# Sample attention of a hybrid decoder step: all scores of a pair of sequences ahead of its products with the values

## The chip, the cores and the metric

The kernel runs on one core of one Trainium2 chip. The metric is the device time of one execution in microseconds (us). A core has five engines with an instruction queue each: TensorE (PE in the profile, its weight loads are PEld), VectorE (DVE), ScalarE (ACT), GpSimd (POOL) and SyncE (SP, which only starts transfers here). POOL starts transfers too.

## What is computed

One step of a one-layer decoder trunk, for a prompt of 1024 tokens and for 8 sample sequences of 8 tokens each that have 2048 tokens of past. In the layer, gated linear attention stands beside sparse attention with three branches per query: compressed blocks, selected blocks and a sliding window. What matters here is the sparse attention of the samples, cut to its core:

```python
p_c = masked_softmax(q @ kc.T - slope * d_c, d_c >= 0)             # compressed blocks
o_c = p_c @ vc
idx = top_k(score_of_blocks(p_c), 16)                               # which blocks are selected
p_s = masked_softmax(q @ k_slc[idx].T - slope * d_s, d_s >= 0)      # selected blocks
o_s = p_s @ v_slc[idx]
p_w = masked_softmax(q @ k_win.T - slope * dist, 0 <= dist <= 512)  # banded keys
o_w = p_w @ v_win
o = gate_c * o_c + gate_s * o_s + gate_w * o_w
```

After it come the output projection, norms and a squared-ReLU MLP of width 4096.

## The kernel before

A first phase makes the conditioning vectors and compresses the keys and values of the samples' past. The main phase normalises, projects, runs the linear attention and then the sparse attention of the prompt in four parts of two tiles of 128 queries, in the order 1, 0, 2, 3. After it come the output projection and the MLP.

The prompt's attention (`branch` and `values` in the attention function) computes, per tile, group of heads and branch, scores on TensorE into the PSUM banks called "dn" (L1185, L1186), adds the mask and takes the maximum on VectorE (L1188), the exponential on ScalarE (L1192), scales on GpSimd (L1198), transposes the weights on TensorE into the banks called "g" (L1209), copies them out on ScalarE (L1211) and multiplies them with the values on TensorE (L1217).

The samples' attention is written out between these steps. `main_phase` keeps a generator, `between`, of sample work; after each piece of prompt work it takes from it until its share of 126 steps is reached. A number that the sample code yields is the weight of what it has just written. After part 2 all that is left is taken. Each instruction's place in its engine's queue is then fixed by the framework's scheduler when the kernel is built: it goes by the order in the program and by its own model of when each instruction is ready. At run time each engine works through its queue strictly in that order.

The samples are taken in four pairs. For a pair, the 128 rows are 2 sequences x 2 key heads x 4 query heads x 8 tokens. `sample_attention` loads for it the compressed values (vc, L1416), the banded keys and values (wk, L1418, and wv, L1420) and 32 pages of selected keys and values in eight units, two for each quarter q (`load_pages`, with the transfers at L247, half of them on SP's queue and half on POOL's). Then:

- the banded scores W (128 x 576): a product that writes the distances (L1362), four with the queries (L1364), the addition with the maximum on VectorE (L1374);
- their softmax (L1368 to L1371: a multiplication on VectorE, the exponential on ScalarE, two small operations on VectorE) and the scaling by the gate (L1433, L1434);
- the product of the compressed weights PC with vc, and of W with the banded values. `weigh` does each: transposes on TensorE into a bank (L1401), a copy to PT on ScalarE (L1403), products on TensorE (L1407) that add up in the bank `po`;
- the scores S of the selected blocks (128 x 2112) in four quarters of 512 and one rest of 64, each as for W, and their softmax with an exponential over 2112 columns;
- the products of S with the values, one rest and four quarters, into the other half of `po`;
- the sum of both halves, O (L1470, L1471), a transpose (L1473) and copies to `cats` (L1478).

All banks of the sample code come from the tag "mm", of which there are two. `po` holds one of them from its first product to O. The units for wk, wv and pages are nine slots that are taken in turn (seven of the weight buffers wr, wh and wl, and two called su): the banded keys of the next pair get the slot that the banded values of this pair leave, and the next banded values the slot of this pair's first page unit. vc has one buffer.

Of the kernel before, what the change touches and what calls it, by code (L numbers as in the profile page):

```python
# [223 lines left out]
class Prog:  # L224
# [6 lines left out]
    def t(self, pool, shape, dt=F32, tag=None, bufs=None):  # L231
        self.n += 1
        kw = {} if bufs is None else {"bufs": bufs}
        return pool.tile(list(shape), dt, name=f"{tag}_{self.n}", tag=tag, **kw)
# [104 lines left out]
    def C(self, name):  # L339
        o, n = self.at["cst"][name]  # L340
        return self.cst[:, o:o + n]
# [1035 lines left out]
    def sample_attention(self, pool):  # L1377
        nc, a, C = self.nc, self.a, self.C2
        t = lambda shape, tag, bufs=1, dt=F32: self.t(pool, shape, dt, tag, bufs)
        slots = cycle(["", "su", "", "", "", "su", "", "", ""])  # L1380


        def unit():
            return t([128, 1024], "su", 2) if next(slots) else self.raw_unit()


        def load_pages(pr, q):
            us = []
            for b2 in range(2):
                u = unit().rearrange("p (g n) -> p g n", g=4)  # L1390
                for g in range(4):
                    self.page_load(u[:, g], a["ckv"], (2 * pr + b2) * 16 + 4 * q + g, nc.gpsimd if g % 2 else nc.sync)
                us.append(u)
            return us

        def weigh(out, P, items, first, last):
            k = len(items)
            w = P.shape[1] // k
            pt = self.bank("mm")[:w, :128 * k]
            for g in range(k):  # L1400
                nc.tensor.transpose(pt[:, 128 * g:128 * g + 128], P[:, w * g:w * g + w], self.C("ident"))  # L1401
            PT = t([128, 512], "PT", 2)[:w, :128 * k]
            nc.scalar.copy(PT, pt)  # L1403

            for g, v in enumerate(items):
                for b2 in range(2):
                    nc.tensor.matmul(out[64 * b2:64 * b2 + 64], PT[:, 128 * g + 64 * b2:128 * g + 64 * b2 + 64], v(b2),  # L1407
                                     start=first and g == 0, stop=last and g == k - 1)

        lt = self.R2("l_t")  # L1410
        zero = C("zero")
        for pr in range(4):
            mx, sm = t([128, 3], "mxs", 2), t([128, 2], "sms", 2)
            new = self.R2("oh_tok")[:, 128 * pr:128 * pr + 128], self.R2("r_new")
            vc = t([128, 2, 128], "vc")
            nc.sync.dma_start(vc, self.vcs[2 * pr:2 * pr + 2].rearrange("b p c -> p b c"))  # L1416
            wk, wv = (unit().rearrange("p (b n) -> p b n", b=2) for _ in range(2))
            nc.sync.dma_start(wk, a["swk"][2 * pr:2 * pr + 2].rearrange("b p t -> p b t"))  # L1418
            wv = wv.rearrange("p b (g d) -> p b g d", g=4)
            nc.sync.dma_start(wv.rearrange("p b g d -> p (b g) d"),  # L1420
                              a["swv"][2 * pr:2 * pr + 2].rearrange("b (g p) d -> p (b g) d", p=128))
            pages = [load_pages(pr, q) for q in range(4)]

            W = t([128, 576], "Ws", 1)
            ps = self.bank("mm")
            self.scores(ps, pr, lambda b2: wk[:, b2], lt, self.R2("r_win"))
            self.add_max(W[:, :512], ps, zero.to_broadcast([128, 512]), None, mx[:, 0:1])
            ps = self.bank("mm")[:, :64]
            self.scores(ps, pr, lambda b2: self.kn[1], *new)
            self.add_max(W[:, 512:], ps, zero.to_broadcast([128, 64]), mx[:, 0:1], mx[:, 2:3])  # L1430
            yield 4
            self.softmax(W, mx[:, 2:3], sm[:, 1:2])
            nc.vector.tensor_tensor(sm[:, 1:2], sm[:, 1:2], self.G[:, pr, 2:3], op=OP.mult)  # L1433
            nc.vector.tensor_scalar(W, W, sm[:, 1:2], None, op0=OP.mult)  # L1434

            po = self.bank("mm")[:, :256].rearrange("p (a n) -> p a n", a=2)
            weigh(po[:, 1], self.PC[:, pr], [lambda b2: vc[:, b2]], True, False)
            yield 1
            weigh(po[:, 1], W[:, :512], [lambda b2, g=g: wv[:, b2, g] for g in range(4)], False, False)
            weigh(po[:, 1], W[:, 512:], [lambda b2: self.vn[1]], False, True)  # L1440
            yield 2

            S = t([128, 2112], "Ss", 1)
            pen = self.pen[:, pr]
            for q in range(4):
                ps = self.bank("mm")
                self.scores(ps, pr, lambda b2: pages[q][b2][:, :, :128], lt,
                            self.R2("r_slc")[:, None, :].to_broadcast([128, 8, 64]))
                self.add_max(S[:, 512 * q:512 * q + 512].rearrange("p (b i) -> p b i", i=64),
                             ps.rearrange("p (b i) -> p b i", i=64),  # L1450
                             pen[:, 8 * q:8 * q + 8, None].to_broadcast([128, 8, 64]),
                             mx[:, 0:1] if q else None, mx[:, 0:1])
                yield 2
            ps = self.bank("mm")[:, :64]
            self.scores(ps, pr, lambda b2: self.kn[0], *new)
            self.add_max(S[:, 2048:], ps, pen[:, 32:33].to_broadcast([128, 64]), mx[:, 0:1], mx[:, 1:2])
            self.softmax(S, mx[:, 1:2], sm[:, 0:1])
            nc.vector.tensor_tensor(sm[:, 0:1], sm[:, 0:1], self.G[:, pr, 1:2], op=OP.mult)
            yield 3
            weigh(po[:, 0], S[:, 2048:], [lambda b2: self.vn[0]], True, False)  # L1460
            for q in range(4):
                items = [lambda b2, q=q, g=g: pages[q][b2][:, g, 128:] for g in range(4)]
                weigh(po[:, 0], S[:, 512 * q:512 * q + 512], items, False, q == 3)
                yield 2
            O = t([128, 64], "O", 1)
            for b2 in range(2):
                for h in range(2):
                    s = slice(64 * b2 + 32 * h, 64 * b2 + 32 * h + 32)
                    c = slice(64 * h, 64 * h + 64)
                    nc.vector.tensor_scalar(O[s], po[s, 0, c], sm[s, 0:1], None, op0=OP.mult)  # L1470
                    nc.vector.tensor_tensor(O[s], O[s], po[s, 1, c], op=OP.add)  # L1471
            pt = self.bank("mm")[:64, :128]
            nc.tensor.transpose(pt, O, self.C("ident"))  # L1473
            for par in range(2):
                for b2 in range(2):
                    src = pt.rearrange("p (b h g r t) -> p b r (h g) t", b=2, h=2, g=2, r=2)[:, b2, par]
                    c = (2 * pr + b2) * 8
                    nc.scalar.copy(self.cats[64 * par:64 * par + 64, :, c:c + 8], src)  # L1478
            yield 1
# [349 lines left out]
```

## Time and profile before

| | |
|---|---|
| median of 3 runs | 1873.94 us (1870.25 to 1876.29) |
| the profiled execution | 1874.2 us |
| its span in the trace | 1872.5 us |
| PE busy | 1779.7 us, 95% of the span |
| DVE, ACT, POOL busy | 60%, 51%, 18% |
| mean granted TensorE clock | 0.976 of full speed |

The profile's page gives the busy time of each engine, then the span in 40 slices of 46.8 us. Its other views answer for a stretch: the busy time of each engine with the granted clock, the instructions in order of time, who waited for whom, and groups of instructions by line and shape. TensorE's clock has two levels, 1.2 and 2.4 GHz; a granted clock of 0.50 in a stretch is the lower one throughout, 1.00 the higher. A PE that is busy at the lower level does about half the work.

### The profile page before, as it was taken

What the parts mean: (1) busy time and instruction counts of PE and PEld (TensorE: products, weight loads), DVE (VectorE), ACT (ScalarE), POOL (GpSimd) and SP (SyncE); (2) the same over time, 40 slices, a digit from 0 to 9 for tenths busy, and PEclk for the clock granted to TensorE, in tenths of its full rate; (3) what the DMA queues carried; (4) which work ended last, traced back from release to release, by engine and by line L of the source; (5) the groups of instructions that cost most, each with busy time, mean ns of one, the idle gap of its engine ahead of it and who ended that gap; (6) DMA issues with size and microseconds to landing.
All of it is one profiled execution on the core that took longest, in us unless ns stands there. A gap on an engine that the chain in (4) does not pass through costs nothing.

```text
span 1872.5 us, 33307 instructions
## 1 busy us (share of the span) xinstructions
PE 1779.7 (95%) x12054; PEld 1626.9 (87%) x12054; DVE 1130.4 (60%) x2528; ACT 952.0 (51%) x1931; POOL 334.6 (18%) x502
## 2 busy tenths in 40 slices
PE   5899989999999999998998899999999999999998
PEld 4688889999989766665796899999999999999998
DVE  6777866474434764554636566855656569665555
ACT  5334445364233767664846556643443365654454
POOL 3534210012401446443312000000000001000000
PEclk9999999999999988998999899999999999999999
DMA  7777451013455513323222366321112145564442
GB/s 247 250 250 255 155 165 58 24 47 129 147 199 174 162 60 99 95 83 113 72 67 85 114 193 202 101 90 57 59 66 90 57 159 184 193 208 152 151 147 96
DMA packets 116779, 246.04 MB, mean 131 GB/s; under 512 B 14443, under 2 KB 71581, under 8 KB 115814
## 3 DMA queue, kind: packets, MB, share of 16 engines
q1 hardware_dynamic: 101046, 197.04, 33.0%
q0 software_dynamic: 13328, 43.99, 6.9%
q10 hardware_dynamic: 2240, 2.88, 0.4%
q8 instruction: 95, 1.56, 0.3%
q14 instruction: 70, 0.57, 0.1%
HBM read 215.94 MB, written 32.05 MB: 132 GB/s over the span
## 4 chain that ended last, share of the span: by engine, by line
PE 76%; DVE 8%; DMA 7%; ACT 3%; issue 3%; SPq 1%; POOL 1%; POOLq 0%; DVEq 0%; ACTq 0%
PE mm L261 11%; PE mm L262 11%; PE mm L263 11%; PE dn L261 5%; PE dn L262 5%; PE dn L263 5%; PE g L1209 3%; PE g L262 3%; PE g L263 3%; PE g L261 3%; PE av L1217 3%; DMA xt<-xT 2%; PE dn L1185 2%; PE dn L1186 2%; PE mm L1407 1%
## 5 line engine op out<-in xcount | busy, mean ns | idle before, releaser
L256 DVE TENSOR_TENSOR wl<-wr,wh 128x1024 fp32r<-128x1024 f32 x174 | 212.9, 1225 | 204.3 <-ACT wh L255 202.8
L255 ACT CAST wh<-wr 128x1024 fp32r<-128x1024 f32 (+1 forms) x176 | 183.3, 1043 | 241.0 <-PE mm L262 106.9
L261 PE MATMUL dn<-fh,wh 128*128 128x384 f32 (+1 forms) x616 | 205.0, 334 | 2.9 <-DVE fo L1627 1.7
L262 PE MATMUL dn<-fl,wh 128*128 128x384 f32 (+1 forms) x616 | 204.0, 331 | 0.0
L263 PE MATMUL dn<-fh,wl 128*128 128x384 f32 (+1 forms) x616 | 203.8, 332 | 0.0
L261 PE MATMUL mm<-hT,wh 128*128 128x384 f32 (+1 forms) x384 | 129.0, 336 | 11.3 <-ACT zq L778 5.2
L262 PE MATMUL mm<-hT,wh 128*128 128x384 f32 (+1 forms) x384 | 127.4, 332 | 0.0
L263 PE MATMUL mm<-hT,wl 128*128 128x384 f32 (+1 forms) x384 | 126.8, 332 | 0.4 <-DVE wl L256 0.4
L261 PEld LDWEIGHTS dn<-fh,wh 128*128 128x128 f32 x616 | 116.2, 189 | 5.5 <-DVE fo L1627 2.9
L262 PEld LDWEIGHTS dn<-fl,wh 128*128 128x128 f32 x616 | 116.3, 189 | 0.3 <-DVE fl L256 0.3
L263 PEld LDWEIGHTS dn<-fh,wl 128*128 128x128 f32 x616 | 116.1, 189 | 0.1
L1627 DVE TENSOR_TENSOR fo<-fo,dn 128x384 f32<-128x384 f32 (+1 forms) x134 | 72.4, 541 | 56.3 <-PE dn L263 56.0
L1211 ACT COPY pw<-g 128x512 f32<-128x512 f32 x148 | 80.7, 586 | 46.1 <-PE g L1209 45.6
L607 POOL TENSOR_TENSOR rs_r<-rs_m,mhalf 128x2 f32<-128x2 f32 (+2 forms) x11 | 11.2, 1019 | 483.3 <-DVE rs_m L606 483.3
L261 PE MATMUL mm<-w1h,wh 128*128 128x256 f32 x256 | 76.7, 300 | 17.7 <-ACT wh L255 16.1
L1185 PE MATMUL dn<-KK,QS 128*128 128x512 f32 (+3 forms) x192 | 77.7, 409 | 11.6 <-DVE mx L1188 10.9
L261 PEld LDWEIGHTS mm<-hT,wh 128*128 128x128 f32 x384 | 73.1, 190 | 14.3 <-ACT zq L778 5.6
L261 PE MATMUL mm<-cth,wh 128*128 128x256 f32 (+1 forms) x256 | 76.9, 302 | 5.3 <-ACT cth L255 5.2
L263 PE MATMUL mm<-x2h,wl 128*128 128x320 f32 x256 | 79.2, 309 | 0.0
L261 PE MATMUL mm<-x2h,wh 128*128 128x320 f32 x256 | 79.2, 309 | 0.0
L262 PE MATMUL mm<-x2l,wh 128*128 128x320 f32 x256 | 79.1, 309 | 0.0
L262 PE MATMUL mm<-ctl,wh 128*128 128x256 f32 (+1 forms) x256 | 76.6, 300 | 0.1
(643 smaller groups left out, 5444.3 us busy)
## 6 DMA issues: line engine op xcount, KB each, us to landing
wr<-w_up SPq DMA_DIRECT2D x72, 512.0 KB, 3.6
wr<-w_down SPq DMA_DIRECT2D x72, 512.0 KB, 3.6
wr<-w_ada SPq DMA_DIRECT2D x48, 512.0 KB, 5.1
wr<-w_f SPq DMA_DIRECT2D x24, 512.0 KB, 3.8
wr<-cw SPq DMA_DIRECT2D x16, 512.0 KB, 5.2
wr<-w_out SPq DMA_DIRECT2D x16, 512.0 KB, 3.5
raw<-cc SPq DMA_DIRECT2D x62, 128.0 KB, 4.8
raw<-cc POOLq DMA_DIRECT2D x61, 128.0 KB, 5.3
```

What stands on the lines that cost most here:

```text
L255: return (self.nc.scalar.copy(h, src), (lo or self.nc.vector).tensor_tensor(l, src, h.bitcast(F32), op=OP.subtract))
L256: (lo or self.nc.vector).tensor_tensor(l, src, h.bitcast(F32), op=OP.subtract))
L261: mm(out, ah, bh, start=start, stop=False)
L262: mm(out, ah, bl, start=False, stop=False)
L263: mm(out, al, bh, start=False, stop=stop)
L1185: nc.tensor.matmul(ps, q, K[:, 0, c:c + cw], start=True, stop=False)
L1186: nc.tensor.matmul(ps, q, K[:, 1, c:c + cw], start=False, stop=True)
L1209: nc.tensor.transpose(pt[:, 128 * g:128 * g + 128], S[g][:, c:c + 128], self.C("ident"))
L1211: box["group"].append((V, pw, nc.scalar.copy(pw, pt)))
L1217: m = nc.tensor.matmul(box["av"][64 * j:64 * j + 64], V, pw.rearrange("p (a j q) -> p j a q", a=2, j=2)[:, j], start=box["first"], stop=en ...
L1407: nc.tensor.matmul(out[64 * b2:64 * b2 + 64], PT[:, 128 * g + 64 * b2:128 * g + 64 * b2 + 64], v(b2), start=first and g == 0, stop=last an ...
L1627: nc.vector.tensor_tensor(o, o, ps, op=OP.add)
```

## The change

Seven lines move. The bank `po` is taken, and the products of the compressed weights and of the banded weights with their values are written, only after the softmax of the selected blocks' scores, right ahead of the products of S with the values. The scores S of a pair so come directly behind its banded scores and their softmax. No instruction is added or removed, and the weights that are yielded stay the same; only their order changes.

```diff
             nc.vector.tensor_scalar(W, W, sm[:, 1:2], None, op0=OP.mult)
 
-            po = self.bank("mm")[:, :256].rearrange("p (a n) -> p a n", a=2)
-            weigh(po[:, 1], self.PC[:, pr], [lambda b2: vc[:, b2]], True, False)
-            yield 1
-            weigh(po[:, 1], W[:, :512], [lambda b2, g=g: wv[:, b2, g] for g in range(4)], False, False)
-            weigh(po[:, 1], W[:, 512:], [lambda b2: self.vn[1]], False, True)
-            yield 2
-
             S = t([128, 2112], "Ss", 1)
             pen = self.pen[:, pr]
             for q in range(4):
...
             self.softmax(S, mx[:, 1:2], sm[:, 0:1])
             nc.vector.tensor_tensor(sm[:, 0:1], sm[:, 0:1], self.G[:, pr, 1:2], op=OP.mult)
             yield 3
+
+            po = self.bank("mm")[:, :256].rearrange("p (a n) -> p a n", a=2)
+            weigh(po[:, 1], self.PC[:, pr], [lambda b2: vc[:, b2]], True, False)
+            yield 1
+            weigh(po[:, 1], W[:, :512], [lambda b2, g=g: wv[:, b2, g] for g in range(4)], False, False)
+            weigh(po[:, 1], W[:, 512:], [lambda b2: self.vn[1]], False, True)
+            yield 2
             weigh(po[:, 0], S[:, 2048:], [lambda b2: self.vn[0]], True, False)
             for q in range(4):
```

## Rows read from the trace of the kernel before

**Rows 1.** Page: busy time of PE; busy tenths and clock in 40 slices.
```profile
PE 1779.7 (95%) x12054; PEld 1626.9 (87%) x12054; DVE 1130.4 (60%) x2528; ACT 952.0 (51%) x1931; POOL 334.6 (18%) x502
...
PE   5899989999999999998998899999999999999998
...
PEclk9999999999999988998999899999999999999999
```

**Rows 2.** Stretches: length, then busy us (instructions) of PE, PEld, DVE, ACT, POOL; clock; DMA.
```profile
715.00:735.00 20.00, 18.80 (x105) 15.10 (x103) 11.99 (x66) 17.65 (x59) 9.46 (x20) 0.66 0.05 14
...
800.00:815.00 15.00, 12.97 (x95) 9.16 (x97) 10.95 (x51) 9.06 (x29) 11.40 (x20) 1.00 0.53 159
```

**Rows 3.** The same view in steps of 5 us at the fourth pair's scores.
```profile
860.00:865.00 5.00, 1.87 (x18) 0.88 (x14) 2.82 (x7) 1.23 (x3) 4.70 (x6) 1.00 0.42 135
865.00:870.00 5.00, 3.46 (x25) 2.90 (x26) 0.68 (x3) 0.84 (x2) 0.00 (x0) 0.63 0.14 46
870.00:875.00 5.00, 5.00 (x18) 2.29 (x17) 0.23 (x1) 0.00 (x0) 0.00 (x0) 0.50 0.33 107
875.00:880.00 5.00, 5.00 (x29) 2.48 (x28) 1.65 (x8) 2.64 (x5) 0.00 (x0) 0.84 0.01 2
...
885.00:890.00 5.00, 4.04 (x25) 2.96 (x23) 3.59 (x16) 2.65 (x4) 1.06 (x3) 1.00 0.00 0
890.00:895.00 5.00, 3.68 (x19) 2.34 (x19) 3.93 (x17) 4.93 (x12) 0.93 (x2) 1.00 0.01 3
```

**Rows 4.** Order of time, POOL, DVE and ACT, fourth pair: start, length, instruction, idle before.
```profile
853.23 2.12 POOL L247 DMA_DIRECT2D wr<-ckv  x4
...
859.74 3.88 POOL L1198 TENSOR_SCALAR Ss<-Ss,sm,gates 128x768 f32<-128x768 f32 x4
...
861.55 2.07 DVE L1368 TENSOR_TENSOR mxs<-mxs,cols 128x1 f32<-128x1 f32 x1
...
863.57 1.13 POOL L247 DMA_DIRECT2D wl<-ckv  x2
...
863.66 0.87 ACT L1369 ACTIVATE Ws<-Ws,mxs,cols 128x576 f32<-128x576 f32 x1 [1.87 <-DVE mxs L1368]
...
865.23 0.52 DVE L1434 TENSOR_SCALAR Ws<-Ws,sms 128x576 f32<-128x576 f32 x1
```

**Rows 5.** Order of time, PE: banded values of the first pair, then the fourth pair.
```profile
701.64 1.09 PE L1407 MATMUL mm<-su,PT 128*64 128x128 f32 x16
...
865.81 0.66 PE L1401 MATMUL mm<-cst,Ws 128*128 128x128 f32 x4 [3.52 <-DVE Ws L1434]
867.19 1.97 PE L1407 MATMUL mm<-wr,PT 128*64 128x128 f32 x16 [0.73 <-ACT PT L1403]
...
883.73 0.50 PE L1362 MATMUL mm<-cstr 128*128 128x512 f32 x1
...
884.65 0.59 PE L1364 MATMUL mm<-wl,Q 128*64 128x512 f32 x1
```

**Rows 6.** Waits, 690 to 925 us: total us, times, longest; PE, then its weight loads.
```profile
PE mm L1401 <- DVE Ws L1434: 3.5, 1, 3.5
...
PEld mm L1362 <- DVE mxs L1374: 0.4, 1, 0.4
```

**Rows 7.** Groups by line and shape, 690 to 925 us: count, busy us, mean ns, idle.
```profile
L1374 DVE CUSTOM_DVE_ANT_1 Ss<-mm,pen,mxs 128x512 f32<-128x512 f32 x12 | 9.0, 751 | 19.6 <-PE mm L1364 19.6
...
L1369 ACT ACTIVATE Ss<-Ss,mxs,cols 128x2112 f32<-128x2112 f32 x4 | 8.6, 2142 | 0.0
```

**Rows 8.** Instructions on the tile mxs: ns min/median/max, first and last start.
```profile
L1368 DVE TENSOR_TENSOR mxs<-mxs,cols x8: 150/156/2072, 695.7 to 887.5; 128x1 f32<-128x1 f32 x8
```

**Rows 9.** Transfers issued, 690 to 925 us: count, size of one, median us to landing.
```profile
wl<-ckv POOLq DMA_DIRECT2D x12, 128.0 KB, 4.1
```

**Rows 10.** Order of time: the second pair's banded keys, on SP, then their scores, on DVE.
```profile
703.56 0.40 SPq L1418 DMA_DIRECT2D su<-swk  x1
...
751.89 0.69 DVE L1374 CUSTOM_DVE_ANT_0 Ws<-mm,cols 128x512 f32<-128x512 f32 x1 [1.23 <-PE mm L1364]
```

## The prediction

> **What bounds the kernel now.** I read the page's busy times first: PE is busy 1779.7 of 1872.5 us [rows 1]. So an edit that moves work without removing any can only pay where PE stands still or runs at its lower clock, 1.2 GHz. The page's slices say where that is: near the start, and around the 16th to 23rd slice, some 700 to 1075 us, where PE's tenths and its clock dip [rows 1]. The softmaxes of the four pairs of samples start between 695.7 and 887.5 us [rows 8], inside that part. Three views of it follow. The stretches show how much PE lacks: 2.03 of 15 us at 800 to 815, a granted clock of 0.66 at 715 to 735 [rows 2], and, at the fourth pair, 4.67 idle us between 860 and 870 and a lower clock up to about 877 [rows 3]. The waits give names: the longest wait of PE on a sample operation is one of 3.5 us, of the transposes of W for the scaled W; on the bank of the scores it waits 0.4 us in all [rows 6]. The order of time shows how the 3.5 us arose [rows 4, 5]: the small multiplication L1368 took 2.07 us, the exponential of W 0.87, the scaling 0.52, and PE, whose next instruction was the transpose of W, stood from 862.3 to 865.8. The clock then fell: sixteen products that took 1.09 us in the first pair took 1.97 [rows 5].
>
> **The change part by part.**
>
> *What moves.* Per pair 6 transposes, 24 products and 3 copies go from ahead of the selected scores to behind their softmax. At 1.09 us for sixteen products [rows 5] the 30 PE instructions are about 2.0 us of PE per pair. None is added, so PE's sum stays.
>
> *The fourth pair's wait.* With the change the next sample work behind the banded scores is the selected scores, which need neither the softmax of W nor `po`. A quarter takes PE 1.51 us (883.73 to 885.24) [rows 5]. With `po` not yet taken, two banks are free once W's two additions are done, before 861.55, so two quarters, 3.0 us, fit into the hole at once; the last of their pages were issued on POOL from 853.23 on [rows 4]. The hole is 10 - 1.87 - 3.46 = 4.67 us [rows 3]. Bounds: 3.0 to 4.67 gained if they start at once, 0 if they don't. I take 3.8, between the two quarters and the whole, because a third can follow once L1368 is over (863.62) and one addition of 0.75 done [rows 4, 7], from 864.4 on.
>
> *The lower clock behind it.* The share at 1.2 GHz is twice what the clock lacks: 3.7, 5.0 and 1.6 us of the three steps from 865, 10.3 us in all [rows 3]. 0.73 of it is idle [rows 5]; the other 9.6 at the ratio 1.97 / 1.09 = 1.81 would take 5.3, so 4.3 us are at stake. Bounds 0 (the clock falls anyway) to 4.3. I take two thirds, 2.9: what went before the fall was the hole, and some of a hole may stay.
>
> *The wait for the exponential of S.* It takes 2.14 us [rows 7], and around the fourth pair's PE idles 0.96 + 1.32 = 2.28 us [rows 3]. The moved products, 2.0 us, now lie ready there. But these gaps are short waits of the prompt's scores for their banks. Bounds 0 to 2.0; I take 0.7.
>
> *A new wait.* The copy of the compressed weights to PT stood beside the exponential of W (0.87 us); now it may stand behind that of S (2.14). Behind it on ACT queue the prompt's copies L1211 and exponentials; on PE the products L1407 wait for it, and all prompt work behind them. Bounds 0 to 2.14 per pair. I take 0.5 in all: the copies of the banded weights showed waits of that size [rows 5].
>
> *Three other pairs.* Their W softmax has no long wait on PE (the 3.5 us is one wait of one) [rows 6], so taking the weights away from there gains nothing. Scores of 1.51 us PE per 0.75 us DVE [rows 5, 7] fill PE as well as the products did: 0, bounds -1 to +1 us.
>
> *The first pair's slow clock.* From 715 to 735 us the lower level covers 13.6 us, but ACT is busy 17.65 of 20 us [rows 2], so a full clock could give back at most 2.35 us. Bounds 0 to 2.35; I take 0, as the exponentials of the prompt stay.
>
> *Two banks.* The selected scores now alternate between two. The row says that PE waited 0.4 us for that bank [rows 6], since prompt work fills the time: 0. The Trainium skill, "Perfetto Trace Analysis", section "Optimizing Tensor Performance", asks that independent groups rotate through different banks, so that taking one out overlaps the next; were each wait exposed, the time would be that of the second rival below, and the row speaks against it.
>
> *Queues.* The next pair's banded keys wait for the slot of this pair's banded values. In the first pair they were issued at 703.56 and used only at 751.89 [rows 10]. They will now be issued behind the selected scores, some 20 us later, which leaves over 20 us of cover. Behind them on SP stands the load of the next banded values, which waits for the products of S with the values anyway. The next vc is loaded later by as much and used later by as much. POOL's page loads keep their order. Cost 0; without the cover it would be a landing, some 4 us [rows 9].
>
> **The sum**, against the profiled execution of 1874.2 us (0.3 above the median of the runs shown, span 1872.5, 1.7 outside it): -3.8 - 2.9 - 0.7 + 0.5 = -6.9, so 1867.3; I say 1867. What is gained at 865 us reaches the end if the stages behind stay bound by PE, which the slices of nine tenths and the clock near one say [rows 1].
>
> **The rivals.**
>
> *The hole moves.* The 2.07 us of L1368, against a median of 0.156 [rows 8], end at 863.62, as does POOL's scaling that began at 859.74 [rows 4]. That doesn't go away, and the additions for the selected scores now stand behind it on DVE. Two quarters run, the third from 864.4 to 865.9. The last quarter's page was issued on POOL behind the same scaling, the second of two at about 864.1; with 4.1 us to landing [rows 9] it is there at 868.3. PE then lacks sample work for 2.4 us, where it lacked it for 3.5, and the clock falls as before: -1.1 - 0.7 + 0.5, so 1873. The prompt's work can't fill it at once, as part 2's last weights are scaled on POOL until 863.62 [rows 4] and have to be transposed, copied and multiplied after that. By the Trainium skill, "SBUF — State Buffer", section "Who interferes with whom", a VectorE operation with two SBUF inputs and a GpSimd operation that reads SBUF shut each other out for a whole instruction; by that rule the trace agrees, with the 2.07 us.
>
> *Every bank wait was exposed.* Sixteen scores, four per pair, wait for the addition before them, 0.75 us each [rows 7]: 12 us, so 1862. For it speaks that DVE waited 19.6 us in these additions for PE [rows 7], so the chain of scores is in series; against it the 0.4 us [rows 6].
>
> *Slower: copies behind the long exponential.* If the scheduler puts the copy of the compressed weights behind the exponential of S in ACT's queue and the products next on PE, each pair costs 2.14 us [rows 7]: 8.6 us. It decides from the point where PE has no prompt work between the two. With the 3.8 us kept and the clock not: 1874.2 + 8.6 - 3.8 = 1879.0, and 1882.8 if the hole stays. For it: ACT is the busiest engine in the first pair, 17.65 of 20 us [rows 2]; against: the queue is laid out with a model of these times, and the longest such wait now is 0.73 us [rows 5].
>
> **How the numbers follow.** Forecast 0.47 (its own range 1861 to 1872), the hole moves 0.28, exposed banks 0.07, slower 0.18. A measurement of this kernel can tell about 0.3%, 5.6 us, from no change, so faster is below 1868.3 us. Two thirds of the forecast's chance lie there, 0.31, with the exposed banks and a rest of the second case 0.41; same 0.41; slower 0.18. Range: at the low end all bounds of the forecast, 4.67 + 4.3 + 2.0 + 2.35 = 13.3, so 1861; at the high end the slower case between its two prices, 1881.
>
> **What would show it.** Right: in the fourth pair PE goes from the banded scores to selected scores without a wait over 1 us, the wait of the transposes of W for L1434 is gone, the granted clock stays near 1.00 where it was 0.63, 0.50 and 0.84, and the pair ends earlier. Wrong: a wait of PE at L1407 or L1401 for PT copies behind L1369; a wait for a page; another stretch of lower clock elsewhere, since the queues of all engines are laid out anew from the first pair on, and a shift of a prompt tile against a pair may open a hole that no row of before shows.

## The result, and the profile after

The changed kernel takes 1864.66 us (median of six runs, 1863.48 to 1869.22), the kernel before 1875.84 beside it (six runs, 1870.25 to 1876.69). The ratio is 0.9945, 95% interval 0.9928 to 0.9961: 10.3 us less, 7.3 to 13.5. The forecast was 1867; the profiled execution fell from 1874.2 to 1863.61 us, by 10.6, where the sum said 6.9. From here on, us of a ratio are of 1876. One of the ten runs of an experiment below, with the banded products alone moved, took 3833.66 us and is left out of every figure.

The page after, its rows of PE and of the granted clock:

```profile
span 1862.0 us, 33308 instructions
...
PE 1773.2 (95%) x12054; PEld 1618.1 (87%) x12054; DVE 1128.9 (61%) x2528; ACT 950.3 (51%) x1931; POOL 339.7 (18%) x502
...
PE   5999989999999899999998899999999999999998
...
PEclk9999999999999999999999999999999999999999
```

The same 12054 matmuls keep PE busy 6.5 us less than before [rows 1]. No work went, so I put this down to the clock, though the profile doesn't separate it from other causes; two profiles with the same order of instructions, below, differ by up to 2.6 us in it. The other 4.0 of the 10.5 us of span are idle time. The eights in the clock's row are gone. The stretches that the prediction read, after (length, busy us of PE, PEld, DVE, ACT, POOL, clock, DMA):

```profile
715.00:735.00 20.00, 18.88 (x148) 14.61 (x150) 10.80 (x61) 18.02 (x67) 12.41 (x25) 0.91 0.18 57
800.00:815.00 15.00, 15.00 (x95) 8.53 (x94) 8.04 (x37) 6.76 (x19) 7.76 (x13) 1.00 0.23 73
...
850.00:855.00 5.00, 5.00 (x27) 2.11 (x25) 4.17 (x18) 3.54 (x10) 4.51 (x6) 1.00 0.30 90
855.00:860.00 5.00, 5.00 (x28) 2.56 (x24) 3.92 (x15) 2.15 (x4) 0.00 (x0) 1.00 0.10 33
860.00:865.00 5.00, 5.00 (x33) 2.82 (x32) 2.37 (x9) 4.47 (x8) 0.72 (x1) 1.00 0.02 5
865.00:870.00 5.00, 4.35 (x34) 2.65 (x32) 1.45 (x7) 2.17 (x5) 3.15 (x4) 1.00 0.00 0
870.00:875.00 5.00, 4.98 (x50) 3.48 (x49) 0.00 (x0) 3.48 (x8) 0.00 (x0) 1.00 0.32 107
```

Two things differ from [rows 2, 3]. Around the fourth pair's scores PE has no hole and the clock stays at 1.00. And at the first pair, where I had booked nothing, the granted clock is 0.91 and not 0.66: 3.4 us at the lower level (by the same view in steps of 5 us) in place of 13.6. PE in order of time at the fourth pair, and the exponentials that belong to it on ACT:

```profile
849.78 0.47 PE L1362 MATMUL mm<-cstr 128*128 128x512 f32 x1
850.18 1.08 PE L1364 MATMUL mm<-wl,Q 128*64 128x512 f32 x4
...
852.49 0.39 PE L1362 MATMUL mm<-cstr 128*128 128x512 f32 x1
```

```profile
853.54 0.87 ACT L1369 ACTIVATE Ws<-Ws,mxs,cols 128x576 f32<-128x576 f32 x1
...
863.82 2.15 ACT L1369 ACTIVATE Ss<-Ss,mxs,cols 128x2112 f32<-128x2112 f32 x1
```

The first selected quarter starts at 852.49, ahead of the exponential of W. From the one exponential to the other it is 10.3 us; before it was 25.0 (863.7 to 888.7). In the other three pairs it was 21.2, 23.6 and 27.8 and is 16.4, 14.4 and 12.6. The waits of PE after, 690 to 925 us (total, times, longest):

```profile
PE dn L1185 <- DVE mx L1188: 3.1, 7, 0.8
PE g L1209 <- POOL Ss L1198: 1.8, 4, 0.6
PE g L1209 <- POOL Sw L1198: 1.6, 2, 1.4
PE mm L1473 <- DVE O L1471: 1.4, 1, 1.4
PE mm L1407 <- ACT PT L1403: 0.3, 1, 0.3
```

The transposes of W wait no more [rows 6]. New are 3.4 us behind GpSimd's scaling of the prompt's weights. Two more rows, the small multiplications and the additions of the selected scores with their idle time before them:

```profile
L1368 DVE TENSOR_TENSOR mxs<-mxs,cols x8: 158/158/197, 695.3 to 863.6; 128x1 f32<-128x1 f32 x8
```

```profile
L1374 DVE CUSTOM_DVE_ANT_1 Ss<-mm,pen,mxs 128x512 f32<-128x512 f32 x12 | 9.0, 750 | 10.4 <-PE mm L1364 10.4
```

The 2072 ns of [rows 8] are gone, and DVE waits 10.4 us for scores where it waited 19.6 [rows 7].

### The profile page after: what moved, and what is told of

Same layout as the page of the kernel before. It is cut to its first block, busy times and chain, and to the rows that moved or that the text cites. A ratio compares the mean times of both kernels' runs of the same rounds, so it can differ in the third digit from the quotient of the medians.

```text
span 1862.0 us, 33308 instructions
## 1 busy us (share of the span) xinstructions
PE 1773.2 (95%) x12054; PEld 1618.1 (87%) x12054; DVE 1128.9 (61%) x2528; ACT 950.3 (51%) x1931; POOL 339.7 (18%) x502
## 4 chain that ended last, share of the span: by engine, by line
PE 75%; DMA 9%; DVE 7%; ACT 3%; issue 2%; POOL 2%; SPq 1%; POOLq 0%; DVEq 0%; ACTq 0%
PE mm L261 11%; PE mm L262 11%; PE mm L263 11%; PE dn L261 5%; PE dn L262 5%; PE dn L263 5%; PE av L1217 3%; PE g L263 3%; PE g L262 3%; PE g L261 3%; PE g L1209 3%; DMA xt<-xT 2%; PE dn L1185 2%; PE mm L1364 2%; PE dn L1186 1%
```

## Experiments

All were timed beside the kernel before. One profile can lie up to 6 us from its kernel's median, so the profiles are read for what they hold, and the times for what it is worth.

### One part of the pairs only

The new order in the fourth pair alone, in the first three, in the first, in the second and third: the moved lines stand twice, under a condition.

```diff
+            if not (pr == 3):
                 po = self.bank("mm")[:, :256].rearrange("p (a n) -> p a n", a=2)
...
             yield 3
+            if pr == 3:
+                po = self.bank("mm")[:, :256].rearrange("p (a n) -> p a n", a=2)
...
```

> Only the fourth pair has the new order; the first three keep the old one, and all queues up to the fourth pair are those of before. If the gain is the fourth pair's hole and the lower clock behind it (my theory): most of it is here, 6 to 9 us faster than before (near 1868), and the wait of the transposes of W for L1434 is gone. If the gain comes from the first three pairs (earlier ends of the pairs, the first pair's slow clock): 0 to 2 us.

> Only the first three pairs have the new order; the fourth has the old one. My theory: the hole of the fourth pair stays, so 0 to 3 us faster than before (1873 to 1876). If the gain comes from pairs that end earlier against the prompt's work: most of the 10 us, and no hole although the fourth pair's order is the old one.

> Only the first pair has the new order. In the first batch the new order in the first three pairs alone gave the whole gain (0.9948), and in its trace the lower clock at the first pair was gone (0.6 in place of 13.6 us of it behind 700 us) and the fourth pair's hole too. New theory: the first pair's lower clock is worth some 5 us, in spite of a busy ACT, and the first pair's own order ends it: 4 to 6 us faster than before, under 4 us of lower clock between 700 and 740, hole of the fourth pair unchanged. If ACT bounds that stretch, as predicted: 0 to 2.4 us.

> Only the second and third pairs have the new order. If they bring the fourth pair earlier against the prompt's tiles and its hole closes by that: 4 to 5 us faster, no idle stretch behind the fourth pair's banded scores, and the first pair's lower clock of 10 to 14 us stays. If they do nothing by themselves: within 1 us of before.

| new order in | median us | ratio, 95% interval | us |
|---|---|---|---|
| fourth pair | 1870.30 | 0.9978 (0.9961 to 0.9996) | -4.1 |
| first three | 1864.80 | 0.9948 (0.9927 to 0.9969) | -9.8 |
| first | 1874.75 | 0.9989 (0.9970 to 1.0007) | -2.1 |
| second and third | 1869.40 | 0.9962 (0.9943 to 0.9981) | -7.1 |
| all (the change) | 1864.66 | 0.9945 (0.9928 to 0.9961) | -10.3 |

The fourth pair alone gives 4.1 us and the first three, with the fourth's order left as it was, practically all of the gain. The parts don't add up (4.1 + 9.8 is more than 10.3), and the profiles suggest why. With the fourth pair alone, 860 to 870 us, and DVE and PE inside it:

```profile
860.00:870.00 10.00, 8.56 (x44) 3.32 (x44) 6.70 (x20) 1.48 (x6) 6.97 (x10) 1.00 0.50 153
```

```profile
864.18 2.07 DVE L1368 TENSOR_TENSOR mxs<-mxs,cols 128x1 f32<-128x1 f32 x1
```

```profile
863.73 0.50 PE L1362 MATMUL mm<-cstr 128*128 128x512 f32 x1
864.16 0.64 PE L1364 MATMUL mm<-su,Q 128*64 128x512 f32 x1
...
865.17 0.50 PE L1362 MATMUL mm<-cstr 128*128 128x512 f32 x1
865.61 0.64 PE L1364 MATMUL mm<-wl,Q 128*64 128x512 f32 x1
...
866.91 0.50 PE L1362 MATMUL mm<-cstr 128*128 128x512 f32 x1 [0.23 <-DVE mxs L1374]
```

The multiplication is as slow as in [rows 4], and PE works through it, with two quarters and then a third, as the sum had it. With the first three pairs alone there is nothing to work through: the fourth pair stands at another place between the prompt's tiles, and the longest of the eight multiplications takes 209 ns (with the first pair alone 206, with the second and third 326). Between the transposes of PC and those of W, PE has scores and transposes of the prompt to do. The two stretches of the hole, and the transposes of W behind their wait:

```profile
860.00:865.00 5.00, 4.39 (x32) 3.32 (x30) 4.33 (x17) 4.65 (x10) 2.08 (x4) 1.00 0.33 99
865.00:870.00 5.00, 4.01 (x40) 2.83 (x41) 0.84 (x3) 3.47 (x8) 3.86 (x4) 1.00 0.01 3
```

```profile
864.12 0.66 PE L1401 MATMUL mm<-cst,Ws 128*128 128x128 f32 x4 [0.39 <-DVE Ws L1434]
```

The hole is gone in these three kernels as well (first three, first, second and third); PE idles 3.4, 1.3 and 1.3 us from 850 to 900, where it idled 8.2. So the fourth pair's hole could be closed in two ways, and the change does both.

Against the expectations: the fourth pair alone gave less than the 6 to 9 us, though its interval reaches 7.3. With the first three, the hole was expected to stay, and it went. The second and third did as expected, with 13.7 us of lower clock left from 700 to 750, and gained more than the 4 to 5 us. The first pair alone ended its own lower clock, but the hole, expected to stay, went too, and the 4 to 6 us didn't come. Its 715 to 735 and 850 to 900 us:

```profile
715.00:735.00 20.00, 18.67 (x151) 13.94 (x152) 12.13 (x79) 19.88 (x72) 11.76 (x24) 1.00 0.14 47
```

```profile
850.00:900.00 50.00, 48.65 (x372) 33.07 (x371) 26.15 (x111) 32.72 (x79) 24.03 (x37) 1.00 0.34 106
```

Both faults are gone here, for 2.1 us (-1.3 to 5.6): less than the hole alone seems to cost in what follows. The interval reaches that price, and the profile is of one of the faster of ten runs (1870.18 us, against a median of 1874.75), so it may show less of both faults than most runs had. Either way the price of the hole is less certain than the next figures make it look.

### The hole's price by two other ways

The kernel before, with the fourth pair's banded transposes reading constants in place of W (its banded weights are left out of the result), and with the fourth pair's small multiplication on ScalarE:

```diff
-            weigh(po[:, 1], W[:, :512], [lambda b2, g=g: wv[:, b2, g] for g in range(4)], False, False)
-            weigh(po[:, 1], W[:, 512:], [lambda b2: self.vn[1]], False, True)
+            weigh(po[:, 1], (self.cst if pr == 3 else W)[:, :512], [lambda b2, g=g: wv[:, b2, g] for g in range(4)], False, False)
+            weigh(po[:, 1], (self.cst if pr == 3 else W)[:, 512:576], [lambda b2: self.vn[1]], False, True)
```

```diff
-        nc.vector.tensor_tensor(mx, mx, self.C2("s_nslope"), op=OP.mult)
+        if act:
+            nc.scalar.mul(mx, mx, self.C2("s_nslope"))
+        else:
+            nc.vector.tensor_tensor(mx, mx, self.C2("s_nslope"), op=OP.mult)
```

> The order of before, but in the fourth pair the transposes for the banded products read a table of constants in place of W, so they wait for no softmax (the banded weights of that pair are left out of the result). If the 3.5 us wait for W and the clock that falls behind it are the gain: 4 to 8 us faster than before. If the wait only moves to the next thing that PE needs (prompt weights still on POOL, additions on DVE): within 1 us of before, with the idle time of 860 to 870 us kept under another name.

> The order of before, but in the fourth pair the small multiplication L1368 of the banded softmax runs on ACT in place of DVE, away from POOL's scaling. If the 2.07 us of that operation made the hole: the wait for W falls from 3.5 to about 1.6 us, and if the clock then holds, 2 to 6 us faster than before; if the clock falls all the same, 1 to 2 us. If the hole doesn't depend on it: within 1 us of before.

Ratios 0.9976 (0.9954 to 0.9997) and 0.9976 (0.9958 to 0.9994): -4.5 us each. With the fourth pair alone these are three edits at the same place, and they gave 4.1 to 4.5 us. But only the fourth pair's new order takes the hole away. With constants in place of W, PE waits 2.3 us for the copy of their transposes to PT, which stands behind the exponential of W in ScalarE's queue (5.9 us idle and 6.9 at the lower level are left from 850 to 900):

```profile
869.17 1.09 PE L1407 MATMUL mm<-wr,PT 128*64 128x128 f32 x16 [2.27 <-ACT PT L1403]
```

Where the slow multiplication is on ScalarE, PE still waits 1.9 us for the scaled W, and behind it the clock is below 1.00:

```profile
860.00:865.00 5.00, 2.23 (x18) 1.14 (x14) 1.35 (x6) 1.80 (x5) 4.53 (x6) 1.00 0.44 127
865.00:870.00 5.00, 4.75 (x33) 3.53 (x35) 0.00 (x0) 0.46 (x2) 0.00 (x0) 0.66 0.44 147
870.00:875.00 5.00, 4.65 (x28) 2.17 (x27) 1.88 (x8) 2.64 (x5) 0.00 (x0) 1.00 0.01 2
```

How much of the 4.5 us is idle time and how much clock, these intervals (0.6 to 8.6 and 1.1 to 7.9 us) don't settle.

### The bank and the place of the products, apart

First, only the banded products move and the compressed ones stay ahead, so that `po` is held through the scores. Second, the old order, but the result of both products is copied out and the bank given back ahead of the scores.

```diff
-            weigh(po[:, 1], W[:, :512], [lambda b2, g=g: wv[:, b2, g] for g in range(4)], False, False)
-            weigh(po[:, 1], W[:, 512:], [lambda b2: self.vn[1]], False, True)
-            yield 2
...
             yield 3
+            weigh(po[:, 1], W[:, :512], [lambda b2, g=g: wv[:, b2, g] for g in range(4)], False, False)
+            weigh(po[:, 1], W[:, 512:], [lambda b2: self.vn[1]], False, True)
+            yield 2
```

```diff
-            po = self.bank("mm")[:, :256].rearrange("p (a n) -> p a n", a=2)
-            weigh(po[:, 1], self.PC[:, pr], [lambda b2: vc[:, b2]], True, False)
+            pw = self.bank("mm")[:, :128]
+            weigh(pw, self.PC[:, pr], [lambda b2: vc[:, b2]], True, False)
...
+            acc = t([128, 128], "acc")
+            nc.vector.tensor_copy(acc, pw)
...
+            po = self.bank("mm")[:, :128]
```

> As the change, but the compressed products stay ahead of the selected scores, so one of the two banks is held over them as before, while the banded products move. If the order of the scores is what counts (my theory): 7 to 10 us faster than before, like the change. If the second bank for the selected scores is what counts: 0 to 3 us faster.

> The order of the kernel before in all pairs, but the two products with the compressed and the banded values are copied out of their PSUM bank to SBUF (one VectorE copy of 128x128 more per pair), and the bank is given back ahead of the selected scores; the products of S take a bank of their own later. Theory A (about half of the gain of the change comes from the second bank that the selected scores get, in all pairs): the time from a pair's exponential of W to that of S shrinks from 21 to 28 us to 10 to 16 us, as in the changed kernel, and the time falls by 5 us or more, to 1871 or less. Theory B (the gain is from the place of the products: scores come at once, weights are turned much later, and the bank is worth nothing, as the 0.4 us of waiting said): the time from exponential to exponential stays over 18 us and the time stays within 3 us of before, 1873 to 1879; the four copies cost under 1 us. The wait of the fourth pair for its scaled W may be seen in either.

The first gives 0.9976 (0.9958 to 0.9994), -4.5 us, at a median of 1871.57: between the 7 to 10 us of one theory and the 0 to 3 of the other, and its interval reaches into both. The second gives 0.9966 (0.9940 to 0.9991), -6.4 us, at 1866.37. Either is worth something alone, and neither is told apart from the other or from half of the change by these intervals. Their additions of selected scores, first and second:

```profile
L1374 DVE CUSTOM_DVE_ANT_1 Ss<-mm,pen,mxs 128x512 f32<-128x512 f32 x12 | 9.0, 749 | 12.1 <-PE mm L1364 12.0
```

```profile
L1374 DVE CUSTOM_DVE_ANT_1 Ss<-mm,pen,mxs 128x512 f32<-128x512 f32 x12 | 9.0, 751 | 14.6 <-PE mm L1364 14.6
```

Each shortens DVE's wait for scores, 19.6 us before. But that idle time is no price: with the new order in the first pair alone it was 7.2 us, less than in the changed kernel, at a gain of 2.1. With the bank given back, exponential to exponential took 17.2, 14.6, 25.0 and 22.4 us: the first two pairs got shorter by 4.0 and 8.9 us, the other two by 2.8 and 2.6. So of its expectations the time is the bank's, and the shortened chain is there in two pairs of four. What it does rule out is that giving the bank back is worth nothing as an edit. It also moves the fourth pair: its exponential of W comes 147.2 us after the first pair's, where it was 167.8. The slow multiplication is there again (2.02 us at 842.54), and PE waits 1.9 us behind it, for a maximum of the prompt's scores. So how much of the 6.4 us is the bank itself is not shown.

### Is it the place alone?

Each pair's place between the prompt's tiles is set by the share of 126 steps. The kernel before and the changed one, both with 130:

```diff
-STEPS = (SAMPLE_WORK, 16)
+STEPS = (130, 16)
```

> A control: the order of before, with 130 in place of 126 as the number of sample steps that the prompt's progress is mapped to, so each piece of sample work comes a little earlier against the prompt and all queues are laid out anew. If a new layout by itself moves the time: 4 us or more either way. If the gain is that of the new order: within 3 us of before.

> The changed kernel with 130 in place of 126 steps of sample work over the first three parts, so that each pair stands at another place between the prompt's tiles; the same for the kernel before alone moved its time by +0.05%. Theory A (the change helps wherever a pair stands, since its chain of scores gets shorter): 8 to 12 us below the kernel before, 1864 to 1868. Theory B (half of the gain is an accident of how the pairs stand to the prompt's tiles): the gain at this place is 5 us or less, 1871 or more, with a hole or a lower clock at 700 to 900 us that the changed kernel doesn't have.

Both expectations take it that the queues are laid out anew. They are not. In the traces the instructions of PE, ScalarE and GpSimd and the transfers stand in the same order with 130 as with 126, in either kernel; on VectorE a single MEMSET, far behind the samples at 1562 and 1552 us, has changed places with its neighbour. In the kernel before, the exponentials of W follow each other by 59.0, 52.7 and 56.0 us with either number. So these two runs say nothing on the place of the pairs. They are second measurements of the same two kernels, and as such they help. The kernel before against itself gives 1.0005 (0.9983 to 1.0027), and shows both its faults again: 13.6 us at the lower level behind 700 us, and 7.4 idle and 13.6 slow us from 850 to 900. The change, measured again, gives 0.9960 (0.9942 to 0.9978), -7.5 us (4.1 to 10.9), with neither fault: its 715 to 735 and 860 to 870 us are

```profile
715.00:735.00 20.00, 18.67 (x144) 13.56 (x143) 11.89 (x74) 19.11 (x71) 10.79 (x23) 1.00 0.16 48
...
860.00:870.00 10.00, 9.89 (x59) 5.41 (x57) 6.00 (x19) 6.72 (x11) 1.06 (x2) 1.00 0.05 14
```

Theory B, that part of the gain is an accident of how the pairs stand to the prompt's tiles, stays untested: no run here has the same order in all pairs at another place. That other pairs could close the fourth pair's hole without its own order speaks for it in part.

### The small multiplication, in the changed kernel

The line on ScalarE in all softmaxes of the changed kernel:

```diff
-        nc.vector.tensor_tensor(mx, mx, self.C2("s_nslope"), op=OP.mult)
+        nc.scalar.mul(mx, mx, self.C2("s_nslope"))
```

> The changed kernel with the small multiplication ahead of each softmax of the samples on ScalarE instead of VectorE. If the 2.07 us that it once took beside GpSimd's scaling had still cost something in the changed kernel, this would be 1 to 2 us faster than the changed kernel, 1863 to 1865; the rows of the changed kernel, in which the longest of the eight took 0.197 us, say that nothing is left there: the same within 2 us, ratio to the kernel before 0.993 to 0.996.

0.9951 (0.9934 to 0.9969), median 1866.93: nothing left to gain there that this can tell, as the 197 ns said. None of the kernels beats the change.

## Why the prediction was right, and what it mis-sized

The time fell as forecast: by 10.3 us (7.3 to 13.5) and, measured again, by 7.5 (4.1 to 10.9), where the sum said 6.9. That the sum came so near is in part luck. It rests almost wholly on the fourth pair, whose terms of 6.7 us measured 4.1 to 4.5, and the pairs that it booked at nothing make up for that. Step by step:

- **The fourth pair's wait**, -3.8, and **the clock behind it**, -2.9: the mechanism is shown, in the kernel with the fourth pair alone too. From 850 to 900 us PE idles 3.9 us where it idled 8.2, and no time is at the lower level where 10.3 were. But three edits against the wait gave 4.1 to 4.5 us and not 6.7. The term for the clock is the likelier excess: two of the three kept a lower clock, and a wait of 1.9 or 2.3 us, and gave no less. That is argued, since the interval of each holds 6.7.
- **The hole moves** (rival): wrong by its own premise. In the fourth pair alone the 2.07 us were there and PE worked on; no wait for a page came. Its third quarter started at 866.91, after a wait of 0.23 us.
- **Three other pairs**, 0: this is the step that failed. The second and third pair alone gave 7.1 us (3.6 to 10.7), beyond the bound of 1; some 4 us of it can be the fourth pair's hole, which these pairs closed without its new order. I had taken the list of waits of PE for a list of all that could be gained: no long wait on PE, so nothing there. What it doesn't list is the place of a pair. With the new order in other pairs the fourth pair meets other prompt work: from the first exponential of W to the last it is 167.8 us before and 158.1 after. It isn't that the pair comes earlier: with the first pair alone it is 169.3, later than before, and the hole is gone all the same.
- **The first pair's slow clock**, 0: ACT is as busy as it was (18.02 of 20 us, 17.65 before), which was the argument, yet the clock rose to 0.91, and to 1.00 where the first pair alone was changed. The change measured again and the five other kernels that change the first pair's order or give its bank back have 0 to 3.4 us at the lower level from 700 to 750 us; the kernel before measured again and the four that leave the first pair alone have 10.2 to 13.7. Worth: the first pair alone gave -2.1 us (-5.6 to +1.3), inside the bound of 2.35, but in its profile the fourth pair's hole is gone too, so what the clock alone is worth stays open.
- **Two banks**, 0: not borne out. Giving the bank back without moving a product gave 6.4 us (1.7 to 11.3), some of it perhaps by the shift of the fourth pair. The 0.4 us of [rows 6] count only what PE stood still for. My reading, which no run shows by itself, is that the queue had been laid out around the one bank, with other work in between, so that the shortage showed as late scores and not as waits. The 19.6 us that DVE waited, which spoke for the second rival, pointed there, though they don't give the size. The rival's 12 us lie above the interval of the bank alone; the time of the change doesn't rule them out (7.3 to 13.5).
- **The wait for the exponential of S**, -0.7, and **the new wait**, +0.5: in the fourth pair the copy to PT did land behind the exponential (866.44, behind 863.82 to 865.97), and PE had prompt work: its waits for PT fell from 1.1 to 0.3 us. From 865 to 870 us, around that exponential, PE idles 0.65 us. The slower rival did not occur.
- **Queues**, 0: right. The second pair's banded keys are issued 13.2 us later than in [rows 10], not some 20, and used at 747.09, 30 us behind that:

```profile
716.77 0.39 SPq L1418 DMA_DIRECT2D su<-swk  x1
```

- The new waits that the prediction feared came on POOL, 3.4 us for the scaling of the prompt's weights, while the prompt's scores waited 3.1 us where they had waited 6.8: about as much came as went.

What stays open is the cause of the gain beyond the hole: the free bank, the order of the scores and the place of the pairs against the prompt. The first two alone gave about half each, the intervals overlap, and both also shift the pairs; the place was not tried by itself.

## What to carry to other kernels

A list of waits prices what an engine stands still for, and it can miss what a shortage of banks or a late operand costs, where the queue was laid out ahead of time with other work in between; ask what the chain of a stage would take if nothing were in between, and test it on one stage alone before booking zero. An edit in a repeated stage is best run for one repetition at a time: here the part that carried the forecast turned out not to be needed once the others had moved. A stall that comes from two engines meeting by chance can go with an edit elsewhere that shifts one of them, as three did here, or stay, as with the bank given back; its price is then no evidence for a particular edit. And a control that is meant to move the layout has to be compared with the kernel that it controls: 130 in place of 126 moved nothing.

## What the runs showed of the hardware

Each run lists its span and mean granted clock; the time at the lower level is twice what the clock lacks, times the span. Over the 77 runs of the kernel before the clock lay between 0.968 and 0.979, and the time went with it:

```
mean granted clock    runs   mean span, us
0.971 or less           19        1877.9
0.972 to 0.974          33        1874.5
0.975 or more           25        1869.6
```

A straight line through the 77 gives 0.35 us of span for each us at the lower level (0.31 to 0.40; correlation 0.86; 0.30 to 0.40 in each of three batches), less than the 0.45 that the prediction took from 1.97 against 1.09 us for sixteen products. In the two profiles of before and after, PE's busy time is 6.5 us less with 33 us fewer at the lower level, 0.2 for each. The Trainium skill, "TensorE: Matmul & The Clock Gate", section "Terms", puts the penalty at the throttled time times what the clock lacks, one half between these two levels; this kernel's runs show less, by both counts, and the sixteen products come nearest to it.

The same sum over all runs of a kernel sets the lower level beside the gain (us at the lower level, mean of the runs; gain by the ratio):

```
kernel                                   runs   lower level   gain
before                                     77           100      -
before, with 130                           10           100   -0.9
constants for W, fourth pair               10            98    4.5
multiplication on ScalarE, fourth pair     10            92    4.5
second and third pair                      10            91    7.1
first pair                                 10            88    2.1
fourth pair                                10            87    4.1
bank given back                             6            87    6.4
banded products alone moved                 9            82    4.5
first three pairs                           7            77    9.8
change, multiplication on ScalarE           7            77    9.2
change, with 130                           10            72    7.5
change                                      6            68   10.3
```

The 32 us that the change took away would be 11 us at 0.35, about its whole gain, where the prediction had looked at 10 of them; of the 33 us in the two profiles, 22 lie from 690 to 925 us. That the two go together is shown over the whole list, loosely: the second and third pair gained 7.1 us with 9 us fewer. That the clock is the cause of the gain and not, in part, a mark of fewer gaps, is not.

The slow multiplication stood in five profiles (before, before with 130, the fourth pair alone, constants for W, the bank given back), with 2.02 to 2.07 us. In each it began within the second of four scalings on GpSimd, of 0.97 us each and back to back, and ended within 0.02 us of the end of the last: it stood through the rest of the second and two whole ones, where the prediction spoke of a whole instruction. Its median in the kernel before is 0.156 us [rows 8].
